# Attention outputs with queries on partitions, and four modulation blocks computed on VectorE instead of TensorE

## The chip, the cores and the metric

The kernel runs on one core of a Trainium2 chip. The core has engines with instruction queues of their own: TensorE (matmuls; the profile shows the loading of stationary operands apart, as PEld), VectorE (DVE), ScalarE (ACT), GpSimd (POOL) and SyncE (SP), which here issues nearly all DMA transfers. SBUF is the on-chip memory with 128 partitions; matmul results land in PSUM, eight banks of 128 x 512 f32. A matmul takes a stationary operand [k, m], loaded first, and streams a moving operand [k, n] past it; the result is [m, n], m on partitions. The metric is the device time of one execution in microseconds, compared by the median of several runs.

## The reference, cut to what matters

Two layers of a diffusion backbone over 1024 latent tokens (a 16 x 64 grid) and 256 context tokens, width 1024, all f32. In each layer adaptive modulation gives six vectors for latents and six for the context (48 tiles of 128 columns, "blocks" 0 to 11 of 512 columns). Then two head groups run on one input projection: a bidirectional mLSTM (8 heads of 64) and neighbourhood attention (8 heads of 64); an output projection and a squared-ReLU MLP follow.

```python
mod = silu_c @ w_ada[l] + b_ada[l]               # and mod_c from silu_cc
sh1, sc1, g1, sh2, sc2, g2 = jnp.split(mod, 6)   # blocks 0-1, 2-3, 4-5, 6-7, 8-9, 10-11
h = rmsnorm(x, norm1_g[l]) * (1 + sc1) + sh1
y = token_mixers(h @ w_in[l], hc @ w_in[l], ...) # mLSTM and attention
x = x + g1 * (y @ w_out[l])
h = rmsnorm(x, norm2_g[l]) * (1 + sc2) + sh2     # blocks 6 to 9 are first needed here
x = x + g2 * (relu(h @ w_mlp1[l]) ** 2 @ w_mlp2[l])
```

In attention each latent query sees a window of 8 rows and 16 columns, with a bias, and all 256 context keys, under one softmax; context queries (layer 0 alone) see the context keys.

```python
s = concat([q @ k_window + bias, q @ k_ctx])
p = softmax(s)                                   # exp(s - max) / sum
y = p_window @ v_window + p_ctx @ v_ctx
```

## The kernel before, in words

**Stages.** `opening` computes modulation blocks 0 to 3 of layer 0 and the first norm. Then, for each layer, `mixers` runs the mLSTM's keys, values and gates, its outputs (`mlstm_out`, tiles of 256 tokens for each of 4 head pairs) and attention (`na`); `outproj`, `up` and `down` follow. Projections are done as three matmuls on f32 numbers split into a high and a low part (`mm3`, L86 to L88).

**Order.** `opening` runs in the order written. Elsewhere the written order gives only the priorities: a scheduler, with estimates of its own for durations, fixes when each instruction is issued, each engine's queue being in order from then on, and hands out tile buffers. A tile name with `bufs=n` has n buffers; a new tile waits for the release of an older one. PSUM has two banks under the name mm and six under q.

**Modulation blocks.** Blocks 6 to 9 of layer 0 come from `ada` (L150): for each of 16 steps (8 slices of k, two column halves), four 32-column stationary tiles of the silu vectors against 256 columns of weights, in four column strips of the array, accumulated in a q bank, with a copy and four transposes (L175) at the end; its 16 transfers have 512 KB. Blocks 4 and 5 come from `ada_rows`: for each 128-column tile of its blocks and each of the two vectors, one 512 KB transfer of weights (L196, into the tile wada, which has one buffer) and one VectorE multiply-and-reduce over 128 x 1024 (L201), and for each vector one transfer (L193) that spreads the silu vector over the partitions. Both are generators. `tick` moves `self.fill` (from `ada`) on by a step, and once that is done, where it is called with True, `self.rows`. It is called in `project_g`, `project2` (False), `project_j` (True) and `mlstm_tile` (True for token tiles 2 and 4).

**Attention.** For each of 4 head pairs (two heads of 64, on 128 partitions), `na_blocks` yields two context blocks of 128 queries (layer 0 only) and eight latent blocks of 128 queries. `na_block` is a generator of three steps for a block:

1. Scores (L844 context keys, L854 window keys), minimum by a VectorE reduction that also negates and adds the bias (L849, L855), exp on ScalarE with its sum (L859), a reciprocal (L860), and the scaling of the 128 x (256 + window) probabilities (L861), for each of the two heads.
2. Transposes of the probabilities, 128 keys at a time or a window's four rows (L869, L880, L888), and copies out of PSUM (L870 ScalarE, L881 VectorE, L889 ScalarE).
3. The output products (L895): the stationary operand is a head's values [keys, 64], the moving one the transposed probabilities [keys, 128 queries]; head 0 writes partitions 0 to 63, head 1 64 to 127, so the result has channels on partitions. `put` copies it on VectorE (L759, L782) into a tile that is stored for the output projection.

`na` calls them so that a new block's step 1 comes after step 2 of the block two before it, then one group of the next head pair's query and key projection (`na_qk`; for the last pair `ahead`, the start of the output projection), then step 3 of that earlier block. Before all that it runs out `self.fill` and `self.rows`.

Of the kernel before, what the change touches and what calls it, by code (L numbers as in the profile page):

```python
# [10 lines left out]
F32 = mybir.dt.float32  # L11
F32R = mybir.dt.float32r
AF = mybir.ActivationFunctionType
ALU = mybir.AluOpType
# [32 lines left out]
class Kern:  # L47
# [698 lines left out]
    def na_blocks(self, l, pr, need_ctx):  # L746
        nc, d, np_ = self.nc, self.d, self.np_
        o = self.nst[pr]
        vs = self.vscr[l]
        v3 = vs[CTX:T, pr * 128:(pr + 1) * 128].rearrange("(r c) e -> r c e", c=GW)  # L750
        k3 = [o["k"][h][:, CTX:T].rearrange("p (r c) -> p r c", c=GW) for h in range(2)]
        yrow = self.yscr[l][512 + pr * 128:512 + (pr + 1) * 128, :]
        if need_ctx:
            yT = np_.tile([128, 512], F32, name="nyT", bufs=2)
            for qt in range(2):
                q = [o["q"][z][0][:, qt * 128:(qt + 1) * 128] for z in range(4)]

                def put(yp, yT=yT, qt=qt):
                    nc.vector.tensor_copy(yT[:, qt * 128:(qt + 1) * 128], yp)  # L759
                    if qt:  # L760
                        nc.sync.dma_start(yrow[:, 0:CTX], yT[:, 0:CTX])

                yield self.na_block(q, None, o["k"], None, None, None, o["vc"], put)
        for hf in range(2):
            R, r0 = NROWS[hf], ROWS0[hf]
            yT = np_.tile([128, 512], F32, name="nyT", bufs=2)
            for cb in range(4):
                c0, w = COLS[cb]
                nl = R * w
                tb = [np_.tile([128, 640], F32, name="S", bufs=SB) for _ in range(2)]  # L770
                for h in range(2):
                    off = self.toff[(hf, cb)] + h * nl
                    nc.sync.dma_start(tb[h][:, CTX:CTX + nl], d["rpbt"][l, pr, :, off:off + nl])
                vt = np_.tile([128, 3, 128], F32, name="vt", bufs=3)
                for lg in range(3):
                    nr = min(4, R - lg * 4)
                    nc.sync.dma_start(vt[0:nr * w, lg, :], v3[r0 + lg * 4:r0 + lg * 4 + nr, c0:c0 + w, :])
                q = [o["q"][z][hf + 1][:, cb * 128:(cb + 1) * 128] for z in range(4)]
                krhs = [k3[h][:, r0:r0 + R, c0:c0 + w] for h in range(2)]

                def put(yp, yT=yT, hf=hf, cb=cb):
                    nc.vector.tensor_copy(yT[:].rearrange("p (r b c) -> p b r c", r=8, b=4)[:, cb, :, :], yp.rearrange("p (r c) -> p r c", r=8))  # L782
                    if cb == 3:
                        nc.sync.dma_start(yrow[:, CTX + hf * 512:CTX + (hf + 1) * 512], yT[:])

                yield self.na_block(q, krhs, o["k"], (R, w), tb, vt, o["vc"], put)
# [26 lines left out]

    def na(self, l, hi, lo, need_ctx, Wq, accs, last):

        run_all(self.fill)
        run_all(self.rows)
        self.wide = 1
        run_all(self.na_qk(l, 0, hi, lo, need_ctx, Wq, accs))
        self.wide = 0  # L820
        pending = []
        for pr in range(4):
            nxt = self.na_qk(l, pr + 1, hi, lo, need_ctx) if pr < 3 else last
            for blk in self.na_blocks(l, pr, need_ctx):
                if len(pending) == 2:
                    next(pending[0])
                next(blk)
                pending.append(blk)
                next(nxt, None)
                if len(pending) > 2:  # L830
                    run_all(pending.pop(0))
            run_all(nxt)
        for blk in pending:
            run_all(blk)

    def na_block(self, q, krhs, k, Rw, tb, vt, vc, put):
        nc, np_ = self.nc, self.np_
        Pn = []
        nl = Rw[0] * Rw[1] if Rw else 0
        mm = nc.tensor.matmul  # L840
        sc = self.bank()
        for h in range(2):
            for z in range(2):
                mm(sc[:, h * CTX:(h + 1) * CTX], q[2 * h + z], k[h][:, 0:CTX], start=z == 0, stop=z == 1, skip_group_check=True)  # L844
        for h in range(2):
            s = tb[h] if nl else np_.tile([128, 640], F32, name="S", bufs=SB)
            m = np_.tile([128, 2], F32, name="smax", bufs=4)
            zb = self.zero[:].to_broadcast([128, CTX])
            nc.vector.tensor_tensor_reduce(s[:, 0:CTX], sc[:, h * CTX:(h + 1) * CTX], zb, -1.0, 3e38, ALU.add, ALU.min, m[:, 0:1])  # L849
            mx = m[:, 0:1]  # L850
            if nl:
                sl = self.bank()
                for z in range(2):
                    mm(sl[:, :nl].rearrange("p (r w) -> p r w", w=Rw[1]), q[2 * h + z], krhs[h], start=z == 0, stop=z == 1)  # L854
                nc.vector.tensor_tensor_reduce(s[:, CTX:CTX + nl], sl[:, :nl], s[:, CTX:CTX + nl], -1.0, m[:, 0:1], ALU.add, ALU.min, m[:, 1:2])  # L855
                mx = m[:, 1:2]
            sm = np_.tile([128, 1], F32, name="ssum", bufs=4)
            sv = s[:, :CTX + nl]
            nc.scalar.activation(sv, sv, AF.Exp, scale=-1.0, bias=mx, accum_out=sm[:])  # L859
            nc.vector.reciprocal(sm[:], sm[:])  # L860
            nc.vector.tensor_scalar(sv, sv, sm[:], None, ALU.mult)  # L861
            Pn.append(s)
        yield
        tiles = []
        tp = self.bank()
        pc = np_.tile([128, 4, 128], F32, name="pc", bufs=2)
        for h in range(2):
            for a in range(2):
                nc.tensor.transpose(tp[:, (h * 2 + a) * 128:(h * 2 + a + 1) * 128], Pn[h][:, a * 128:(a + 1) * 128], self.ident)  # L869
        nc.scalar.copy(pc[:].rearrange("p a t -> p (a t)"), tp[:])  # L870
        for a in range(2):
            tiles.append((128, [vc[:, a, h * 64:(h + 1) * 64] for h in range(2)], [pc[:, h * 2 + a, :] for h in range(2)]))
        if nl:
            R, w = Rw
            pl = np_.tile([128, 4, 128], F32, name="pl", bufs=2)
            tp = self.bank()
            kw = 4 * w
            for h in range(2):
                for a in range(2):
                    nc.tensor.transpose(tp[:kw, (h * 2 + a) * 128:(h * 2 + a + 1) * 128], Pn[h][:, CTX + a * kw:CTX + (a + 1) * kw], self.ident)  # L880
            nc.vector.tensor_copy(pl[:kw].rearrange("p a t -> p (a t)"), tp[:kw, :])  # L881
            for a in range(2):
                tiles.append((kw, [vt[:kw, a, h * 64:(h + 1) * 64] for h in range(2)], [pl[:kw, h * 2 + a, :] for h in range(2)]))
            k3 = (R - 8) * w
            p3 = np_.tile([128, 2, 128], F32, name="pl3", bufs=2)
            tp = yp = self.bank()
            for h in range(2):
                nc.tensor.transpose(tp[:k3, h * 128:(h + 1) * 128], Pn[h][:, CTX + 2 * kw:CTX + nl], self.ident)  # L888
            nc.scalar.copy(p3[:k3].rearrange("p a t -> p (a t)"), tp[:k3, 0:256])  # L889
            tiles.append((k3, [vt[:k3, 2, h * 64:(h + 1) * 64] for h in range(2)], [p3[:k3, h, :] for h in range(2)]))  # L890
        yp = (yp if nl else self.bank())[:, 256:384]
        yield
        for i, (kw, v, pt) in enumerate(tiles):
            for h in range(2):
                mm(yp[h * 64:(h + 1) * 64, :], v[h], pt[h], start=i == 0, stop=i == len(tiles) - 1, skip_group_check=True)  # L895
        put(yp)


    def load_y(self, l, gi, hi, lo, ks=range(KT)):
# [520 lines left out]
    def mixers(self, l, xsrc, hi, lo, need_ctx, W, accs, Wv):  # L1420
        self.wide = 0
        if l == 0:
            for v in range(2):
                self.nc.sync.dma_start(self.sscr[v, :].rearrange("(k p) -> p k", p=128), self.silu[:, :, v])
            self.fill = self.ada(l, range(6, 10), "q")
            self.rows = self.ada_rows(l, range(4, 6), range(2))
        self.gt, self.mst, self.nst = None, {}, {}
        with self.open(name=f"mix{l}", side="right") as self.mx, self.open(name=f"mkv{l}") as self.mp:
            self.cosT = self.load(self.mx, "cos", [128, 8, 32])
# [274 lines left out]
def run_all(g):  # L1704
    for _ in g:
        pass


def chain(*gs):
    for g in gs:  # L1710
        yield from g
# [138 lines left out]
```

## Time and profile before

| | us |
|---|---|
| median of 3 runs | 2898.99 (2896.84 to 2901.7) |
| the profiled execution | 2898.96 |
| its span, first to last instruction | 2897.0 |
| mLSTM of layer 0, about | 100 to 471 |
| attention of layer 0, about | 471 to 700 |
| attention of layer 1, about | 1976 to 2195 |

All rows shown are from that one execution; the clock that TensorE was granted was 0.997 of full over it. The profile's page gives each engine's busy time; views of the trace give busy time in chosen stretches, groups of instructions by line with the minimum, median and maximum duration in ns, waits (who waited for whom, total us, times, longest), and the timeline (start, duration, engine, line, operation, output<-inputs, shapes, count). A matmul's row names stationary shape and then moving shape, so 128*64 128x128 is 64 stationary columns and 128 moving ones on 128 rows; an f32 product that isn't split beforehand shows as two records, one a pass. Names such as q and mm are the PSUM tiles.

### The profile page before, as it was taken

Reading aid. Unit: us, or ns where it says so; the run is one execution under the profiler, and the core shown is the slowest. Engines: PE = TensorE matmul, PEld = TensorE weight load, DVE = VectorE, ACT = ScalarE, POOL = GpSimd, SP = SyncE. Lnnn points to the kernel's source line nnn. Section 1 sums busy time; section 2 is a strip of 40 time slices with the busy share of each in tenths; the row PEclk is TensorE's granted clock in tenths of the full one; section 3 lists DMA queues with packets and bytes.
Section 4 is the critical chain, followed back from the end, with each engine's and each line's share of the span. In section 5 each row is a group of like instructions: output and inputs, shape, how many; then the busy total and the mean of one; then the engine's idle time right before and its main releaser. Section 6 shows DMA issues by size and latency. Waiting matters only on the chain. (4 is left out here: it accounts for less than half of the span.)

```text
span 2897.0 us, 45725 instructions
## 1 busy us (share of the span) xinstructions
PE 2839.9 (98%) x16644; PEld 2405.4 (83%) x16644; DVE 2217.4 (77%) x5097; ACT 1264.8 (44%) x2426; POOL 67.2 (2%) x117
## 2 busy tenths in 40 slices
PE   7999999999999999999999999999999999999998
PEld 4888888888888888888889988888877788888888
DVE  6678987786698777589878778877775887759774
ACT  5333334564563333344545333335564533334443
POOL 0000000001000000000000000000010000000000
PEclk9999999999999999999999999999999999999999
DMA  7433333236447555798977122223356454478673
GB/s 243 155 114 99 121 106 96 86 120 200 155 154 242 194 193 198 249 338 284 328 260 263 65 83 71 77 71 103 94 160 206 131 178 149 156 246 312 216 250 102
DMA packets 278947, 497.42 MB, mean 172 GB/s; under 512 B 23329, under 2 KB 119585, under 8 KB 278721
## 3 DMA queue, kind: packets, MB, share of 16 engines
q1 hardware_dynamic: 278720, 494.49, 51.8%
q8 instruction: 131, 2.15, 0.3%
q14 instruction: 96, 0.78, 0.1%
HBM read 398.82 MB, written 95.59 MB: 171 GB/s over the span
## 5 line engine op out<-in xcount | busy, mean ns | idle before, releaser
L86 PE MATMUL q<-ah,whi 128*128 128x512 f32 (+1 forms) x1488 | 555.1, 373 | 3.3 <-ACT ah L946 2.2
L88 PE MATMUL q<-ah,wlo 128*128 128x512 f32 (+1 forms) x1488 | 553.4, 372 | 1.2 <-DVE wlo L947 1.1
L87 PE MATMUL q<-al,whi 128*128 128x512 f32 (+1 forms) x1488 | 553.9, 372 | 0.0
L86 PE MATMUL mm<-ah,whi 128*128 128x512 f32 (+1 forms) x1104 | 380.0, 344 | 2.1 <-ACT ah L905 2.0
L88 PE MATMUL mm<-ah,wlo 128*128 128x512 f32 (+1 forms) x1104 | 379.0, 343 | 0.5 <-DVE wlo L81 0.5
L87 PE MATMUL mm<-al,whi 128*128 128x512 f32 (+1 forms) x1104 | 379.0, 343 | 0.0
L86 PEld LDWEIGHTS q<-ah,whi 128*128 128x128 f32 x1488 | 280.3, 188 | 53.8 <-ACT ah L946 3.0
L88 PEld LDWEIGHTS q<-ah,wlo 128*128 128x128 f32 x1488 | 280.3, 188 | 51.3 <-DVE wlo L947 2.3
L87 PEld LDWEIGHTS q<-al,whi 128*128 128x128 f32 x1488 | 280.4, 188 | 49.4 <-issue 1.4
L86 PE MATMUL mm<-whi,ah 128*128 128x512 f32 (+2 forms) x864 | 314.0, 364 | 0.6 <-DVE st L312 0.4
L87 PE MATMUL mm<-wlo,ah 128*128 128x512 f32 (+2 forms) x864 | 310.0, 360 | 0.0
L88 PE MATMUL mm<-whi,al 128*128 128x512 f32 (+2 forms) x864 | 309.1, 358 | 0.0
L86 PEld LDWEIGHTS mm<-ah,whi 128*128 128x128 f32 x1104 | 209.0, 189 | 28.3 <-ACT ah L905 2.6
L88 PEld LDWEIGHTS mm<-ah,wlo 128*128 128x128 f32 x1104 | 209.1, 189 | 25.3 <-DVE wlo L81 1.0
L87 PEld LDWEIGHTS mm<-al,whi 128*128 128x128 f32 x1104 | 209.1, 189 | 24.1
L946 ACT CAST ah<-raw 128x512 fp32r<-128x512 f32 (+1 forms) x264 | 143.2, 567 | 123.4 <-PE q L88 57.8
L86 PEld LDWEIGHTS mm<-whi,ah 128*128 128x128 f32 x864 | 164.2, 190 | 27.5 <-issue 3.2
L88 PEld LDWEIGHTS mm<-whi,al 128*128 128x128 f32 x864 | 164.4, 190 | 23.2 <-issue 0.9
L87 PEld LDWEIGHTS mm<-wlo,ah 128*128 128x128 f32 x864 | 164.6, 190 | 21.9 <-issue 0.2
L947 DVE TENSOR_TENSOR al<-raw,ah 128x512 fp32r<-128x512 f32 (+1 forms) x264 | 158.0, 621 | 25.2 <-ACT ah L946 24.8
L947 DVE TENSOR_TENSOR wlo<-raw,whi 128x1024 fp32r<-128x1024 f32 x84 | 102.4, 1222 | 73.6 <-ACT whi L946 71.0
L86 PE MATMUL q<-th,whi 128*128 128x512 f32 x384 | 150.1, 391 | 2.5 <-DVE s L1111 2.3
(284 smaller groups left out, 5253.7 us busy)
## 6 DMA issues: line engine op xcount, KB each, us to landing
raw<-w SPq DMA_DIRECT2D x168, 512.0 KB
raw<-hid SPq DMA_DIRECT2D x104, 512.0 KB
wada<-w_adaT SPq DMA_DIRECT2D x96, 512.0 KB
wraw<-w SPq DMA_DIRECT2D x80, 512.0 KB
hid<-hb SPq DMA_DIRECT2D x128, 256.0 KB
hid<-ht SPq DMA_DIRECT2D x96, 256.0 KB
gb<-gscr SPq DMA_DIRECT2D x36, 512.0 KB
wada<-w_ada SPq DMA_DIRECT2D x32, 512.0 KB
```

The costliest lines, as they stand in the source:

```text
L86: mm(out, lh, rh, start=start, stop=False, skip_group_check=True)
L87: mm(out, lh, rl, start=False, stop=False, skip_group_check=True)
L88: mm(out, ll, rh, start=False, stop=stop, skip_group_check=True)
L946: ins = self.nc.scalar.copy(hi, src)
L947: self.nc.vector.tensor_sub(lo, src, fview(hi))
```

## The change

In `na_block` the scaling of the probabilities is gone: exp writes the two heads' sums into one tile of two columns. In the output products the transposed probabilities are stationary (128 queries) and the values move (64 columns), so the result has queries on partitions and the two heads side by side in columns. VectorE takes the reciprocal of the two sums once and multiplies the 128 x 128 result by them. A fourth step then transposes that tile on TensorE (one 128 x 128 transpose into a new q bank), and `put` copies it from there as before.

`na` keeps up to four blocks alive: step 2 of the block two before, step 1 of the new one, step 4 of the block three before, the projection group, step 3 of the block two before, and a `tick(True)`.

Blocks 6 to 9 leave `ada`: `self.fill` is empty, and `self.rows` is a chain of blocks 4 and 5 and then 6 to 9, all by `ada_rows`, taken on by the ticks of the mLSTM and of attention; what is left is run out after attention instead of before it.

```diff
@@ na
-        run_all(self.fill)
-        run_all(self.rows)
         self.wide = 1
         run_all(self.na_qk(l, 0, hi, lo, need_ctx, Wq, accs))
         self.wide = 0
-        pending = []
+
+        live = []
         for pr in range(4):
             nxt = self.na_qk(l, pr + 1, hi, lo, need_ctx) if pr < 3 else last
             for blk in self.na_blocks(l, pr, need_ctx):
-                if len(pending) == 2:
-                    next(pending[0])
+                if len(live) > 1:
+                    next(live[-2])
                 next(blk)
-                pending.append(blk)
+                live.append(blk)
+                if len(live) == 4:
+                    run_all(live.pop(0))
                 next(nxt, None)
-                if len(pending) > 2:
-                    run_all(pending.pop(0))
+                if len(live) == 3:
+                    next(live[0])
+                self.tick(True)
             run_all(nxt)
-        for blk in pending:
-            run_all(blk)
+        for _ in range(2):
+            next(live[1])
+            run_all(live.pop(0))
+            next(live[0])
+        run_all(live[0])
+        run_all(self.rows)
@@ na_block
+        sm = np_.tile([128, 2], F32, name="ssum", bufs=4)
...
-            sm = np_.tile([128, 1], F32, name="ssum", bufs=4)
             sv = s[:, :CTX + nl]
-            nc.scalar.activation(sv, sv, AF.Exp, scale=-1.0, bias=mx, accum_out=sm[:])
-            nc.vector.reciprocal(sm[:], sm[:])
-            nc.vector.tensor_scalar(sv, sv, sm[:], None, ALU.mult)
+            nc.scalar.activation(sv, sv, AF.Exp, scale=-1.0, bias=mx, accum_out=sm[:, h:h + 1])
...
         for i, (kw, v, pt) in enumerate(tiles):
             for h in range(2):
-                mm(yp[h * 64:(h + 1) * 64, :], v[h], pt[h], start=i == 0, stop=i == len(tiles) - 1, skip_group_check=True)
-        put(yp)
+                mm(yp[:, h * 64:(h + 1) * 64], pt[h], v[h], start=i == h == 0, stop=i == len(tiles) - 1, skip_group_check=True)
+        nc.vector.reciprocal(sm[:], sm[:])
+        y = np_.tile([128, 2, 64], F32, name="ny", bufs=2)
+        nc.vector.tensor_tensor(y[:], yp.rearrange("p (h e) -> p h e", h=2), sm[:].unsqueeze(2).to_broadcast([128, 2, 64]), ALU.mult)
+        yield
+        tp = self.bank()
+        nc.tensor.transpose(tp[:, 0:128], y[:].rearrange("p h e -> p (h e)"), self.ident)
+        put(tp[:, 0:128])
@@ mixers
-            self.fill = self.ada(l, range(6, 10), "q")
-            self.rows = self.ada_rows(l, range(4, 6), range(2))
+            self.rows = chain(*(self.ada_rows(l, blocks, range(2)) for blocks in (range(4, 6), range(6, 10))))
```

More of the change, by code (lines that the diff above doesn't have):

```diff
@@ L756, in na_blocks, with put @@
                 q = [o["q"][z][0][:, qt * 128:(qt + 1) * 128] for z in range(4)]
-                def put(yp, yT=yT, qt=qt):
-                    nc.vector.tensor_copy(yT[:, qt * 128:(qt + 1) * 128], yp)
+                def put(y, yT=yT, qt=qt):
+                    nc.vector.tensor_copy(yT[:, qt * 128:(qt + 1) * 128], y)
                     if qt:
@@ L779, in na_blocks, with put @@
                 krhs = [k3[h][:, r0:r0 + R, c0:c0 + w] for h in range(2)]
-                def put(yp, yT=yT, hf=hf, cb=cb):
-                    nc.vector.tensor_copy(yT[:].rearrange("p (r b c) -> p b r c", r=8, b=4)[:, cb, :, :], yp.rearrange("p (r c) -> p r c", r=8))
+                def put(y, yT=yT, hf=hf, cb=cb):
+                    nc.vector.tensor_copy(yT[:].rearrange("p (r b c) -> p b r c", r=8, b=4)[:, cb, :, :], y.rearrange("p (r c) -> p r c", r=8))
                     if cb == 3:
```

## The prediction, made before the changed kernel had run

> **What bounds the kernel now.** First the page: how busy each engine is over the span.
>
> ```profile
> span 2897.0 us, 45725 instructions
> PE 2839.9 (98%) x16644; PEld 2405.4 (83%) x16644; DVE 2217.4 (77%) x5097; ACT 1264.8 (44%) x2426; POOL 67.2 (2%) x117
> ```
>
> The profiled execution took 2898.96 us, 1.96 us around its span of 2897.0; the median of three runs is 2898.99 (2896.84 to 2901.7). I sum against 2898.96. TensorE is busy 98% of the span, but matmul ends are modelled, so I looked at the two attention stages alone, where nearly all of the change lies: first the busy time of every engine in each, then whom TensorE waited for (first the stage of layer 0, then that of layer 1; total us, times, longest).
>
> ```profile
> core 0: us, PE busy (x) PEld busy (x) DVE busy (x) ACT busy (x) POOL busy (x), PEclk, DMA share, GB/s
> 471.00:700.00 229.00, 222.66 (x1857) 193.55 (x1856) 179.01 (x586) 135.55 (x316) 14.14 (x14) 1.00 0.37 110
> 1976.00:2195.00 219.00, 214.16 (x1680) 182.13 (x1679) 169.92 (x513) 122.47 (x260) 9.23 (x7) 1.00 0.39 119
> ```
>
> ```profile
> PE q L895 <- ACT pl L889: 2.9, 3, 2.0
> PE q L869 <- DVE S L861: 1.1, 1, 1.1
> ...
> PE q L895 <- ACT pl L889: 1.9, 4, 0.7
> ```
>
> TensorE is idle 229.00 - 222.66 = 6.3 us in the first stage and 219.00 - 214.16 = 4.8 us in the second: 11.2 us in 448. VectorE is at 78% and the only wait of TensorE for the normalisation (L861) is 1.1 us. So TensorE sets the pace of attention, and whatever the change takes off VectorE can give back at most about 11 us. What counts is TensorE time per block. A busy matmul overlaps the next, so I price by the distance between starts.
>
> **The output products (L895).** Today the values are the stationary operand (64 columns) and P the moving one (128 columns); the two heads write the two partition halves. Start, duration, engine, line, shapes, records:
>
> ```profile
> 509.15 0.39 PE L88 MATMUL mm<-ah,wlo 128*128 128x512 f32 x1
> 509.47 0.66 PE L895 MATMUL q<-pc,vc 128*64 128x128 f32 x8
> 509.96 0.83 PE L895 MATMUL q<-pl,vt 128*64 128x128 f32 x12
> 510.71 0.66 PE L869 MATMUL q<-consts,S 128*128 128x128 f32 x4
> 511.21 0.49 PE L880 MATMUL q<-consts,S 128*128 128x128 f32 x3
> ...
> 606.08 0.39 PE L88 MATMUL mm<-ah,wlo 128*128 128x512 f32 x1
> 606.40 0.66 PE L895 MATMUL q<-pc,vc 128*64 128x128 f32 x8
> 606.99 0.66 PE L869 MATMUL q<-consts,S 128*128 128x128 f32 x4
> ```
>
> A latent block has 20 records (5 key tiles, 2 heads, 2 passes for f32). From the end of L88's slot (509.15 + 0.23, the spacing of such matmuls) to L869 at 510.71 is 1.33 us. The four transposes behind it take 0.50 instead of the 0.43 that the row at 221.45 below shows, so a latent block's products cost about 1.39 us. A context block (8 records) costs 606.99 - 606.31 = 0.68, with the same tail 0.74. Twenty records in that time means that the heads run side by side: ten slots of 0.11 and some 0.3 us for going into and out of the halved array.
>
> Afterwards P is stationary with 128 columns, the values move with 64, one head after the other. The trace has that shape almost exactly: the mLSTM's numerator, L646, stationary 128x128, moving 65 columns, f32.
>
> ```profile
> 251.59 0.40 PE L88 MATMUL mm<-whi,al 128*128 128x512 f32 x1
> 251.82 1.90 PE L646 MATMUL q<-kva,P 128*128 128x65 f32 x16
> 253.53 0.48 PE L86 MATMUL mm<-whi,ah 128*128 128x512 f32 x1
> 253.85 0.40 PE L87 MATMUL mm<-wlo,ah 128*128 128x512 f32 x1
> ...
> L646 PEld LDWEIGHTS q<-kva,P x576: 186/192/195, 153.9 to 1956.6; 128*128 128x128 f32 x192
> L895 PEld LDWEIGHTS q<-pc,vc x576: 132/137/137, 475.4 to 2193.6; 128*64 128x64 f32 x192
> ```
>
> Sixteen records take 253.53 - 251.82 = 1.71 us, and the next spacing is 0.32 instead of 0.23: (1.71 + 0.09) / 16 = 0.1125 us each, though 65 moving columns are half of 128. The load of 128 stationary columns (192 ns against 137) seems to set that pace, so the halved moving operand buys nothing. Twenty records make 2.25 us, eight 0.90. Layer 0 has 4 head pairs with 8 latent and 2 context blocks, layer 1 4 with 8: 64 latent, 8 context. **64 x (2.25 - 1.39) + 8 x (0.90 - 0.74) = 55.0 + 1.3 = +56.3 us.**
>
> The Trainium skill, page "TensorEngine Tiling (Array Packing)", section "Performance Considerations", advises for a right side of at most 64 columns to swap stationary and streaming operand and tile the columns twofold; that is the form the change gives up. Its factor of up to 2 would make 2.78 us of 1.39 (an estimate), 64 x 0.53 = 34 us more than my sum; the rows say a factor of 1.6, since the halved array has its own entry and exit.
>
> **The transpose back.** Each block gets one 128x128 transpose, 72 in all.
>
> ```profile
> 221.45 0.60 PE L175 MATMUL q<-consts,wada 128*128 128x128 f32 x4
> 221.88 0.78 PE L646 MATMUL q<-kva,P 128*128 128x65 f32 x6
> ```
>
> Four take 0.43 us, one 0.108: **72 x 0.108 = +7.8 us.** It waits for VectorE's reciprocal and multiply (0.16 + 0.29, below), and everything behind it on TensorE's queue, the next projection first, waits too. In the written order the ten transposes and eight score matmuls of two other blocks lie between, some 2.2 us, so near nothing; at the worst all 72 pay 0.45, +32 us. Nearest to the cover: **+1**.
>
> **The normalisation on VectorE.**
>
> ```profile
> L860 DVE RECIPROCAL ssum<-ssum x144: 134/164/167, 472.5 to 2177.0; 128x1 f32<-128x1 f32 x144
> L861 DVE TENSOR_SCALAR S<-S,ssum x144: 340/504/1055, 473.2 to 2177.7; 128x520 f32<-128x520 f32 x32, 128x608 f32<-128x608 f32 x32, 128x544 f32<-128x544 f32 x32, 128x640 f32<-128x640 f32 x32
> L439 DVE TENSOR_TENSOR ropea<-mm,cos x118: 255/284/292, 75.4 to 1947.1; 128x128 f32<-128x128 f32 x118
> ```
>
> Gone: 144 x (0.164 + 0.504) = 96 us. New: 72 reciprocals (0.16) and 72 multiplies of 128x128 out of PSUM, like L439 (0.29): 32 us. That is 64 us off VectorE, and it shortens the way from exp to the transposes by 0.7 us a head. On the end it is worth only what TensorE waits: bounds 0 and -11.2 us; the larger waits are for ScalarE's copy (L889), which stays, but a slower TensorE gives all of them more cover. **-5 us.**
>
> **Blocks 6 to 9 of the modulation.** Removed from TensorE: 128 records on L150 in batches, and four transposes.
>
> ```profile
> 204.78 0.61 PE L646 MATMUL q<-kva,P 128*128 128x65 f32 x4
> 205.32 1.07 PE L150 MATMUL q<-wada,silu 128*32 128x256 f32 x16
> 206.32 0.50 PE L86 MATMUL mm<-whi,ah 128*128 128x512 f32 x1
> 206.66 0.39 PE L87 MATMUL mm<-wlo,ah 128*128 128x512 f32 x1
> ...
> L201 DVE CUSTOM_DVE_ANT_0 wada<-wada,consts x96: 1252/1279/1286, 243.2 to 1617.6; 128x1024 f32<-128x1024 f32 x96
> L201 DVE DVE_READ_ACCUMULATOR2_ANT mod<- x96: 74/82/89, 244.4 to 1618.8; 128x1 f32 x96
> ...
> SPq L196 <- DVE mod L201: 27.5, 9, 5.2
> SPq L777 <- PE q L869: 49.1, 20, 7.7
> ```
>
> Sixteen records run from 204.78 + 4 x 0.1125 = 205.23 to 206.32, 1.09 us, and the next spacing is 0.11 too long: 1.20. Eight such batches and the transposes (0.43) are 10 us. About four batches lie before 125 us, beside the gates' serial scans, where other work may have to fill in; if they were free, 5 us remain. **-9 us.**
>
> Added on VectorE: 32 reductions of 1.28 + 0.08 = 1.36, 43.5 us. The calls count out to 28 steps in the mLSTM (20 joint projections, 8 tiles; the first 17 are for blocks 4 and 5, as now) and 22 in attention, so of the 32 some 10 and 22: 14 us and 30 us. In layer 0's attention VectorE loses 80 x 0.668 = 53 and gains 40 x 0.45 + 30 = 48: it stays near 174 us, in a longer stage, and covers all of it. In the mLSTM the 16 reductions of today lie at 243 to 414 us beside a full TensorE. I cost them at nothing there; if the cover went, each would show its 1.36 us.
>
> Each step also issues one 512 KB transfer on SP, where there were 16; 34 replace them (32 pieces, two broadcast rows). SP takes its queue in order, and a piece waits for the reduction before it (L196 above, between 240 and 471 us: 9 times, up to 5.2 us); behind it stand the bias loads (L777) and values of later blocks. These already wait 49.1 us for buffers in layer 0's attention (the last row) without TensorE waiting for them. Bytes don't bind: 22 pieces are 11.5 MB, in some 130 us 90 GB/s above the 110 of that stage.
>
> **Sum:** +56.3 + 7.8 + 1 - 5 - 9 = +51; 2898.96 + 51 = **2950 us**.
>
> **Rivals.** (a) *The stationary load does not bind for the new products; faster.* If the moving columns alone set the pace, 64 take half of the 0.108 us that 128 take: 0.054 a record, 1.08 for a latent block, 0.43 for a context block. 64 x -0.31 + 8 x -0.31 + 7.8 + 1 - 5 - 9 = -27.5, **2871 us**. It turns the sign below 0.074 a record, where the sum is zero (64 x 20 + 8 x 8 = 1344 records, 94.9 us of products today, 5.2 of the other terms to pay). One row speaks for it, transposes of the opening with 128 stationary and 64 moving columns:
>
> ```profile
> 33.09 0.43 PE L175 MATMUL mm<-consts,arow 64*128 64x64 f32 x4 [0.88 <-DVE arow L172]
> L175 PE MATMUL mm<-consts,arow x8: 222/223/273, 33.1 to 51.5; 64*128 64x64 f32 x8
> ```
>
> The last of four starts 0.43 - 0.22 = 0.21 us after the first: 0.07 each, which would give -6 us. Against it: these are transposes, one pass; L646 is a two-pass product as here. Chance 0.07. The Trainium skill, page "TensorE: Matmul & The Clock Gate", section "Back-to-back issue gap", gives 81 ns per matmul with its load at 128 moving columns; by it the sum would be about +9, 2908 us (an estimate); L646 at 0.1125 disagrees.
>
> (b) *Slower still: the row pieces hold up attention's queues.* A reduction whose piece is late stops VectorE, and the score reductions behind it stop exp and TensorE. For it: the 9 waits of SP above. If each of the 22 steps shows its 1.28 us, +28: **2978 us**. Against: TensorE hardly waited in the mLSTM with the same steps. It decides once a step waits beyond the 5 to 6 us of a projection between two blocks. Chance 0.12.
>
> (c) *The products cost what I say, but every wait goes and planning improves around them*, including the hidden ones in the mLSTM, where a PSUM bank comes free: -10 - 11 and some 20 more would bring 64 + 1 - 41 = +24, **2923 us**. No row shows 20 us to win. Chance 0.05.
>
> **How the numbers follow.** Forecast 0.76. Its own range: low 64 - 10 - 11 = +43, 2942, less 6 for reordering, 2936; high 64 + 8 - 5 = +67, 2966. For 8 in 10 I go to 2930 and, for (b), to 2980; left out are (a), (c) and the ends of the forecast's own cases, some 0.2. Within 0.2% (5.8 us, about what this kernel's measurement can tell): 0.03, from the near ends of (a) and (c); faster, the rest of (a): 0.05; slower: 0.92.
>
> **What would show it.** The output products as 128x128 stationary with 64 moving columns, 1440 minus missing records, spaced 0.112; attention stages longer by about 33 us (layer 0) and 31 us (layer 1) less their waits; the 128-record group on L150 gone and the mLSTM some 9 us shorter; reductions on the row line x128; VectorE in layer 1's attention down by 30 us. I am wrong if the spacing is near 0.06, if the stages don't grow, or if TensorE waits for the back transpose or VectorE by tens of us.

## The result, and the profile after

The changed kernel takes 2950.86 us, median of four runs (2949.73 to 2959.24), against 2898.35 before (four runs): 1.0184 times as long, 95% interval 1.0171 to 1.0197, or +52.5 us. Forecast were 2950, +51. First the page of the changed kernel, then the busy time of every engine in its two attention stages.

```profile
span 2948.7 us, 45551 instructions
PE 2894.1 (98%) x16584; PEld 2489.8 (84%) x16584; DVE 2198.5 (75%) x5012; ACT 1268.7 (43%) x2426; POOL 67.1 (2%) x117
```

```profile
core 0: us, PE busy (x) PEld busy (x) DVE busy (x) ACT busy (x) POOL busy (x), PEclk, DMA share, GB/s
466.00:727.00 261.00, 254.44 (x1896) 237.94 (x1896) 176.09 (x554) 136.42 (x312) 14.12 (x14) 1.00 0.47 146
2000.00:2244.60 244.60, 243.46 (x1715) 224.59 (x1714) 144.90 (x450) 124.95 (x262) 8.95 (x7) 1.00 0.36 107
```

TensorE is as full as before; its stages are longer. VectorE lost 25 us in layer 1's attention (169.92 to 144.90) and 3 us in layer 0's (179.01 to 176.09), where the row pieces (each one 512 KB transfer of weights and one reduction) took the place of the scaling. To place the stages' ends exactly, here are the first and last start of the score matmuls (L844 before, L851 after) and of the output copies, layer 0 and then layer 1; first the kernel before, then the changed one.

```profile
L844 PE MATMUL q<-nk,nqc x32: 277/282/365, 468.6 to 653.7; 128*128 128x256 f32 x32
L782 DVE COPY nyT<-q x32: 271/290/293, 501.9 to 700.1; 128x128 f32<-128x128 f32 x32
L844 PE MATMUL q<-nk,nq x128: 277/282/384, 1976.4 to 2168.1; 128*128 128x256 f32 x128
L782 DVE COPY nyT<-q x32: 272/291/293, 1997.5 to 2194.7; 128x128 f32<-128x128 f32 x32
```

```profile
L851 PE MATMUL q<-nk,nqc x32: 278/283/384, 463.0 to 670.3; 128*128 128x256 f32 x32
L782 DVE COPY nyT<-q x32: 276/284/292, 502.3 to 726.7; 128x128 f32<-128x128 f32 x32
L851 PE MATMUL q<-nk,nq x128: 274/283/388, 2000.5 to 2214.9; 128*128 128x256 f32 x128
L782 DVE COPY nyT<-q x32: 277/284/290, 2025.3 to 2244.4; 128x128 f32<-128x128 f32 x32
```

Attention of layer 0 begins 5.6 us earlier (468.6, 463.0) and lasts 263.7 instead of 231.5 us, +32.2; that of layer 1 lasts 243.9 instead of 218.3, +25.6. These three make -5.6 + 32.2 + 25.6 = +52.2; the rest of the kernel nets to under 1 us.

The output products, in the timeline of the changed kernel:

```profile
494.62 0.39 PE L88 MATMUL mm<-ah,wlo 128*128 128x512 f32 x1
494.84 1.00 PE L900 MATMUL q<-vc,pc 128*128 128x64 f32 x8
495.68 1.50 PE L900 MATMUL q<-vt,pl 96*128 96x64 f32 x12
497.02 0.61 PE L873 MATMUL q<-consts,S 128*128 128x128 f32 x4
497.46 0.60 PE L884 MATMUL q<-consts,S 128*128 128x128 f32 x4
...
L900 PEld LDWEIGHTS q<-vc,pc x576: 186/192/247, 480.6 to 2241.8; 128*128 128x128 f32 x192
```

Twenty records from 494.84 to 497.02, 2.18 us or 0.109 each, and the transposes behind keep their 0.44: no entry and no exit. Before it was 1.39. The loads take 192 ns, as L646's.

### The profile page after: what moved, and what is told of

Read it like the earlier page. It is cut to its first block, busy times and chain, and to the rows that moved or that the text cites. A ratio compares the mean times of both kernels' runs of the same rounds, so it can differ in the third digit from the quotient of the medians.

```text
span 2948.7 us, 45551 instructions
## 1 busy us (share of the span) xinstructions
PE 2894.1 (98%) x16584; PEld 2489.8 (84%) x16584; DVE 2198.5 (75%) x5012; ACT 1268.7 (43%) x2426; POOL 67.1 (2%) x117
## 5 line engine op out<-in xcount | busy, mean ns | idle before, releaser
L201 DVE CUSTOM_DVE_ANT_0 wada<-wada,consts 128x1024 f32<-128x1024 f32 x128 | 163.5, 1278 | 26.0 <-DMA wada<-w_adaT 25.5
```

The source lines that it names most:

```text
L201: nc.vector.tensor_tensor_reduce(raw, raw, row, 1.0, self.bada[l][:, i:i + 1], ALU.mult, ALU.add, mod[:, i, v:v + 1])
```

## The experiments

### The two parts apart

First the row pieces alone, with attention's blocks as before (parts of the edit):

```diff
 mixers
-            self.fill = self.ada(l, range(6, 10), "q")
-            self.rows = self.ada_rows(l, range(4, 6), range(2))
+            self.rows = chain(*(self.ada_rows(l, blocks, range(2)) for blocks in (range(4, 6), range(6, 10))))
 na
-        run_all(self.fill)
-        run_all(self.rows)
...
                 if len(pending) > 2:
                     run_all(pending.pop(0))
+                self.tick(True)
             run_all(nxt)
         for blk in pending:
             run_all(blk)
+        run_all(self.rows)
```

> The kernel before with only blocks 6 to 9 moved to VectorE steps (ticks in the mLSTM and in attention, the rest run out behind attention); attention's blocks as before. Theory: TensorE loses the 10 us of the tiled products, 5 to 10 of them show: 2889 to 2894. Rival (row pieces hold up attention's queues): 22 pieces cost about 1.3 us each there, 2900 or more.

Measured: 2911.94 us against 2899.67, ratio 1.0039 (1.0025 to 1.0053), +12.3. My theory of this part is wrong; the rival is nearer. Stage ends, engines, whom TensorE waited for, in layer 0's attention:

```profile
L844 PE MATMUL q<-nk,nqc x32: 278/283/582, 462.7 to 666.3; 128*128 128x256 f32 x32
L782 DVE COPY nyT<-q x32: 264/286/293, 496.4 to 712.4; 128x128 f32<-128x128 f32 x32
...
463.00:712.70 249.70, 236.04 (x1876) 199.82 (x1876) 206.73 (x640) 138.03 (x319) 14.30 (x14) 0.98 0.49 152
...
PE q L869 <- DVE S L861: 4.5, 4, 1.8
PE q L854 <- DVE smax L855: 1.9, 1, 1.9
PE q L888 <- DVE smax L849: 1.7, 1, 1.7
```

The mLSTM ends 5.9 us earlier, as in the whole change, but the attention stage takes 249.7 instead of 231.5 us: 22 pieces cost 18 us. VectorE is at 83% there. TensorE now waits for the scaling and for the score reductions and is idle 249.70 - 236.04 = 13.7 us, 7 more than before. The granted clock is lower too, 0.98 over the stage, which is 0.02 of 250 = 5 us. The two make 12 of the 18 us; the other 6 lie inside what the profile counts as busy. Four stretches of 10 us in this run:

```profile
510.00:520.00 10.00, 8.13 (x69) 6.60 (x70) 7.09 (x24) 4.54 (x12) 0.00 (x0) 0.97 0.72 226
520.00:530.00 10.00, 9.43 (x73) 7.68 (x74) 7.64 (x19) 6.11 (x13) 0.00 (x0) 0.86 0.45 146
550.00:560.00 10.00, 8.25 (x54) 7.14 (x53) 8.38 (x22) 5.20 (x13) 0.00 (x0) 0.84 0.60 192
590.00:600.00 10.00, 8.11 (x66) 7.07 (x66) 7.77 (x23) 6.66 (x15) 0.00 (x0) 0.89 0.43 136
```

Where TensorE stood for 1.7 to 1.9 us, that stretch of 10 us or the next shows a clock of 0.84 to 0.89; before and in the changed kernel these four stretches have 1.00. So these waits came with a loss beyond their length.

Then the changed attention alone, with the modulation as before (the diff of the change in `na` and `na_block`, without the `tick` and with the two `run_all` ahead):

> The changed attention, blocks 6 to 9 on TensorE as before. Theory: the swapped products and the transposes cost some 57 to 61 us less a few us of waits, 2951 to 2960, slower than the whole change by what the first run gains. Rival (the products are cheap and the row pieces make the loss): 2915 or less.

Measured: 2953.69, ratio 1.0187 (1.0172 to 1.0202), +54.0. The theory holds: attention makes the whole loss, about 27 us in each layer by the rows below. The row pieces, which cost 12 us by themselves, add nothing to it; the whole change lies 1 to 3 us lower, which the intervals don't tell apart.

```profile
L852 PE MATMUL q<-nk,nqc x32: 278/283/387, 468.4 to 671.6; 128*128 128x256 f32 x32
L782 DVE COPY nyT<-q x32: 277/285/292, 507.3 to 727.3; 128x128 f32<-128x128 f32 x32
L852 PE MATMUL q<-nk,nq x128: 274/283/561, 2002.0 to 2218.3; 128*128 128x256 f32 x128
L782 DVE COPY nyT<-q x32: 276/284/290, 2026.9 to 2247.7; 128x128 f32<-128x128 f32 x32
```

Layer 0's attention takes 258.9 us here and 263.7 with the pieces: 22 pieces cost 5 us, not 18. The change gains about as much ahead of attention, which begins at 463.0 instead of 468.4.

### Is it the load of 128 columns?

```diff
             for h in range(2):
-                mm(yp[:, h * 64:(h + 1) * 64], pt[h], v[h], ...)
+                for u in range(2):
+                    us = slice(u * 64, u * 64 + 64)
+                    mm(yp[us, h * 64:(h + 1) * 64], pt[h][:, us], v[h], ...)
```

> The whole change, but each output product split into two with 64 stationary columns (queries 0 to 63 and 64 to 127), which go to the two halves of the array and of PSUM's partitions; moving operand and result as in the change. Theory (the load of 128 stationary columns sets the pace of 0.112 us a record): a pair side by side takes 0.055 to 0.07, a latent block 1.3 to 1.7 us with the entry into the halves instead of 2.19, the whole 2905 to 2925. Rival (a fixed 0.11 us for every pass of 64 columns, whatever is loaded): no gain, 2950 or more.

Measured: 2920.82, ratio to before 1.0076 (1.0061 to 1.0091), 30 us less than the whole change.

```profile
494.98 0.39 PE L88 MATMUL mm<-ah,wlo 128*128 128x512 f32 x1
495.30 0.69 PE L902 MATMUL q<-vc,pc 128*64 128x64 f32 x16
495.81 0.87 PE L902 MATMUL q<-vt,pl 96*64 96x64 f32 x24
496.62 0.65 PE L873 MATMUL q<-consts,S 128*128 128x128 f32 x4
497.11 0.60 PE L884 MATMUL q<-consts,S 128*128 128x128 f32 x4
```

The theory holds. Forty records run from 495.21 (494.98 + 0.23) to 496.62, 1.41 us; with 0.06 more for the transposes behind, which take 0.49 instead of 0.43, that is 1.47, near the 1.39 of the products before. Moving operand, results and arithmetic are those of the change; only the stationary columns are halved and paired. A pass of 64 moving columns has no fixed 0.11 us: 20 pairs in 1.41 us are 0.07 a pair. The rival is out, and the pace goes by the stationary columns. That it is their load, 138 ns here (L902) against 192, is the likely reading; another cost of the full width isn't separated. Of the 64 x (2.18 - 1.47) = 45 us that TensorE's queue lost, 30 came off the end. Layer 1's attention is 20 us shorter than in the whole change, layer 0's only 13: TensorE is idle for 12.8 us there instead of 6.6, and two of its waits are larger than the 1.7 and 1.2 us of the change:

```profile
PE q L908 <- ACT pc L874: 3.7, 3, 2.4
PE q L861 <- DVE nyT L782: 3.4, 1, 3.4
```

L908 is the transpose back, L861 a score product; with less work ahead of them on TensorE the copies on ScalarE and VectorE come late.

### The transpose back

```diff
-        tp = self.bank()
-        nc.tensor.transpose(tp[:, 0:128], y[:].rearrange("p h e -> p (h e)"), self.ident)
-        put(tp[:, 0:128])
+        put(y[:].rearrange("p h e -> p (h e)"))
```

> The whole change without the transpose back: the scaled tile is copied out as it stands, queries on partitions (left out: the transpose, so attention's output is misplaced). Theory: 72 transposes of 0.108 us and the few us that TensorE waits at them, 7 to 13 us less than the whole change: 2938 to 2944. Rival (the wait for VectorE in front of it is the larger loss): 20 us or more, under 2931.

Measured: 2946.32, 4.5 us less than the whole change by the medians, 6 by the ratios to before (1.0163, 1.0148 to 1.0178, whose interval overlaps that of the change). The rival is out, and my theory's 7 to 13 us look too many, though the overlapping intervals don't exclude 7. Three stretches of this run's second attention:

```profile
2145.00:2160.00 15.00, 13.83 (x92) 11.96 (x90) 10.02 (x26) 8.94 (x17) 3.41 (x3) 1.00 0.59 191
2160.00:2175.00 15.00, 15.00 (x103) 14.94 (x104) 8.30 (x31) 8.69 (x20) 1.69 (x2) 0.77 0.55 167
2205.00:2220.00 15.00, 13.43 (x72) 11.82 (x71) 5.80 (x18) 5.56 (x12) 0.00 (x0) 0.89 0.51 163
```

TensorE stands 1.2 and 1.6 us, and the clock after it costs 15 x 0.23 + 15 x 0.11 = 5 us; this attention lasts 246.4 us (1997.2 to 2243.6), longer than the 243.9 with the transposes. That the clock ate the rest is argued from this one profiled execution. Over the four runs the granted clock doesn't order the times: the one with the highest, 0.996, is the slowest, 2947.18.

### What VectorE's scaling is worth

The kernel before without L860 and L861:

> The kernel before without the reciprocal and the scaling of the probabilities, 96 us of VectorE (left out: attention's output stays unnormalised). Theory: TensorE paces attention, so it is worth at most TensorE's idle time, 0 to 11 us, about 5: 2888 to 2899. Rival (VectorE's normalisation paces attention): 20 us or more, under 2880.

Measured: 2898.00 against 2899.67, ratio 0.9994 (0.9985 to 1.0004). No change.

```profile
471.00:700.00 229.00, 223.81 (x1867) 195.03 (x1866) 140.47 (x427) 134.71 (x316) 14.02 (x14) 1.00 0.38 113
```

VectorE falls from 179.01 to 140.47 us in that stage and TensorE's idle time only from 6.3 to 5.2. The same two lines left out of the kernel with the row pieces of the first experiment:

> The kernel before with blocks 6 to 9 as in the first run (22 pieces in attention, 2912), but without reciprocal and scaling of the probabilities (left out: the output stays unnormalised). Theory (the 18 us are VectorE's load: its 22 reductions delay the score reductions): with 53 us off VectorE most of them go, 2894 to 2901. Rival (SP's queue or the transfers' landing holds attention up): still 2907 or more.

Measured: 2901.55 against 2899.14, ratio 1.0013 (1.0003 to 1.0022): 8 us less than with the scaling by the ratios, 10 by the medians, and just above my theory's range. The ends of layer 0's attention say how far the theory goes:

```profile
L844 PE MATMUL q<-nk,nqc x32: 278/283/387, 459.5 to 650.8; 128*128 128x256 f32 x32
L782 DVE COPY nyT<-q x32: 272/292/293, 492.5 to 698.5; 128x128 f32<-128x128 f32 x32
```

The stage lasts 239.0 us, 10.7 less than with the scaling (249.7). But without scaling and without pieces, in the run before this one, it lasts 228.9 (468.4 to 697.3), so 22 pieces still cost 10 us here, where they cost 18 with the scaling. The time of the whole kernel doesn't show it, because attention begins 9 us earlier than in the kernel before. So about 8 of the 18 us were VectorE's scaling. Whether the other 10 are the rest of VectorE's work, the transfers' landing or SP's queue is open. The ends are those of one profiled execution, 2895.73 us, 6 below this median.

### Where else the pieces could go

In the mLSTM alone, two steps a tick, none in attention: first in the changed kernel, by the edit below, then in the kernel before, with the same `tick` and, as in the first experiment, the chain in `mixers` and `run_all(self.rows)` behind attention instead of the two `run_all` ahead.

```diff
 tick
-            next(self.rows, None)
+            for _ in range(2):
+                next(self.rows, None)
 na
-                self.tick(True)
```

> The whole change with two row steps a tick in the mLSTM and none in attention, so that blocks 6 to 9 are done by the mLSTM's end. Attention of layer 0 took 264.3 us with the pieces and 259.5 in the run with the changed attention alone. Theory (pieces cost 5 us in attention, nothing in the mLSTM, where 16 of them cost nothing before): 2943 to 2948. Rival (the mLSTM's VectorE, 83% busy, can't take 32 more reductions): 2951 or more, with TensorE's idle time in the mLSTM up.

Measured: 2986.24, ratio to before 1.0303 (1.0287 to 1.0318), 35 us more than the change.

> The kernel before, blocks 6 to 9 moved to VectorE, all steps in the mLSTM (two a tick), attention untouched. Theory: the 5.6 us by which attention of layer 0 began earlier stay, the 18 us of the pieces in attention go: 2892 to 2897, and it beats both kernels. Rival (the mLSTM pays for the pieces instead): 2900 or more.

Measured: 2930.22, ratio to before 1.0109 (1.0094 to 1.0124), +31. My theory is wrong in both; the mLSTM pays. Its middle, in the kernel before and in the second of these runs, and whom TensorE waited for in that run:

```profile
125.00:440.00 315.00, 312.45 (x1941) 258.15 (x1938) 268.25 (x1027) 104.82 (x286) 16.30 (x35) 1.00 0.37 119
```

```profile
125.00:440.00 315.00, 296.24 (x1643) 241.12 (x1643) 282.23 (x1001) 93.24 (x255) 18.88 (x33) 0.94 0.44 146
...
PE mm L88 <- DVE wlo L82: 6.7, 3, 2.6
PE mm L87 <- DVE ropeb L440: 5.5, 4, 2.3
```

Idle time grows from 2.6 to 18.8 us, and the clock of 0.94 takes 19 us more of 315: together 35 us. That is the delay of attention: with 22 more pieces in the mLSTM it begins at 498.8 instead of 462.7 (the first experiment), and in the changed kernel at 497.5 instead of 463.0. VectorE's busy share alone doesn't tell it: in the changed kernel's row it is as high (281 us against 282), with ten pieces instead of 32 and TensorE hardly waiting.

```profile
125.00:440.00 315.00, 312.73 (x1867) 260.76 (x1868) 281.31 (x1055) 105.19 (x284) 16.54 (x35) 0.99 0.36 115
```

One step at each of the mLSTM's ticks instead, the rest as in the second of these runs:

```diff
 tick
-        if next(self.fill, self) is self and rows:
-            next(self.rows, None)
+        next(self.rows, None)
```

> The kernel before, blocks 6 to 9 moved to VectorE, one step at every tick of the mLSTM (47 of the 50 steps, the False ticks too), instead of two at some, which took 2930. Theory (VectorE's load in the mLSTM is the cause: 32 reductions beside 268 us of work in 315): still 2912 to 2930. Rival (the cause was two steps at once, the second waiting for its transfer): 2900 or less.

Measured: 2914.22, ratio 1.0045 (1.0028 to 1.0062). Within the theory's range; but half of the loss of the run before went, so the pairing, or the places of the ticks, had its share too. Three of the 32 pieces come behind attention here.

```profile
125.00:440.00 315.00, 306.43 (x1801) 254.36 (x1802) 286.13 (x1035) 101.49 (x274) 16.19 (x34) 0.97 0.43 140
```

Last, the kernel before with the 22 pieces that the mLSTM leaves written behind attention (the first experiment without its `tick`):

> The kernel before, blocks 6 to 9 moved to VectorE, one step a tick in the mLSTM as in the change, none in attention's loop; the 22 that are left are written behind attention, so they rank behind its work and fill what VectorE has left there and in the output projection. Theory (what costs is a reduction that comes ahead of score reductions while VectorE is 75 to 90% busy): the tiled products' 6 to 9 us stay gained and attention loses little, 2891 to 2900. Rival (a piece costs wherever it lands, by SP's queue or by the second norm waiting for it): 2905 or more.

Measured: 2921.68, ratio 1.0074 (1.0059 to 1.0089). The rival holds.

```profile
755.00:785.00 30.00, 23.86 (x91) 18.54 (x91) 16.12 (x22) 9.04 (x12) 0.00 (x0) 0.83 0.85 277
815.00:845.00 30.00, 24.16 (x125) 20.69 (x125) 19.50 (x33) 18.32 (x33) 0.00 (x0) 0.89 0.40 139
...
PE mm L268 <- ACT ssq L271: 6.1, 1, 6.1
...
SPq L196 <- DVE mod L201: 39.6, 15, 7.1
```

The 22 pieces share one buffer and run one after the other from 693.9 to 822 us, through the output projection; in the first of these stretches the DMA engines are 85% busy. TensorE stands twice for 6 us at the second norm (L268), and the clock is 0.83 and 0.89 in the two stretches. Attention itself takes what it took before (231.9 us). That the norm's chain waits for these pieces, rather than for the transfers that they delay, isn't separated.

No version that computes the whole output beats the kernel before.

## Why the prediction was right, point by point

The sum was right within 2 us, and its main term was the right one. That it came so near is luck: four terms were off, in both directions, and cancelled. By the stages, products 51, transposes 8, waits -6.5, the modulation -5.6 and the pieces +5 make the 52 that was measured; the last of these had been put at nothing.

- **TensorE sets the pace of attention.** Right. Taking 39 us off VectorE in one stage changed nothing measurable.
- **Products, +56.3.** The halves show that the stationary columns set the pace. The size is 64 x (2.18 - 1.39) = 51 with little for the context blocks: I had carried over L646's exit of 0.09, which is there in front of a split matmul but not in front of transposes. There were 1344 records, as my first rival counts them; the 1440 among the signs was a slip.
- **The rule on tiling.** The Trainium skill's "TensorEngine Tiling (Array Packing)", section "Performance Considerations", was right in direction for this case: the form that it advises was the faster. The "Up to 2×" in the page's "Theoretical Speedup" is 2.18 / 1.39 = 1.57 here. The swap itself isn't needed for it: the products of the change with their stationary columns in halves took 1.47.
- **Transposes, +7.8 and +1 of waiting.** At 0.11 each they are there, and TensorE waited 1.8 us for their input in layer 0 and not in layer 1. Left out, they gave back 4.5 us; the clock may hide the rest, which isn't shown.
- **Waits given back, -5.** TensorE's idle time in the two stages fell from 6.3 + 4.8 to 3.1 + 1.5 us with the changed attention alone, -6.5; in the whole change it is 6.6 + 1.1, the pieces having put 3.5 back in layer 0.
- **The modulation's products off TensorE, -9.** Measured 5.6 at attention's start, near the bound of 5 that I gave. Three of the eight batches, not four, begin before 125 us (88.6, 107.4 and 123.4). In the changed kernel TensorE stands behind them and the clock falls, 15 x 0.11 = 1.7 us (the same stretch before: 1.9 us of waits for the same tile, full clock), as this stretch and its wait show:

```profile
125.00:140.00 15.00, 13.68 (x59) 10.95 (x60) 11.50 (x40) 3.30 (x8) 0.00 (x0) 0.89 0.59 183
...
PE q L516 <- DVE vw L514: 1.9, 1, 1.9
```

Two other runs with the same modulation in the mLSTM have no idle time and full clock in this stretch: the pieces behind attention, where attention begins at 461.8, and the pieces without scaling, at 459.5, 6.8 and 9.1 us earlier than before. So up to the whole 9 was there to win; why the stop came in some runs and not in others isn't shown.
- **Row pieces at nothing.** This step failed. In the changed attention 22 cost 5 us, with the scaling still there 18. I had written that VectorE, near 174 us in the stage, covers all of it; 176 was right, the cover not whole. The price without cover, 1.36 each, was too high in attention (18 / 22 = 0.8) and too low in the mLSTM, where 22 more took 35 us, 1.6 each, half of it clock.
- **Rivals.** (a), the fast one, fell with the first rows: 0.11 a record, not 0.054. (b) was priced for queues; its place, attention of layer 0, was right, its size 5 us instead of 28. Of its cause only the share of VectorE's scaling is shown, 8 of 18 us. (c) did not happen.

The two parts are not additive: +54.0 for attention, +12.3 for the pieces, +52.5 together. The relief of VectorE was worth nothing alone, and to the pieces about 8 us without the scaling and 13 in the change, where TensorE's longer stage covers them too.

## What to carry to other kernels

Where TensorE is full, price a swap of stationary and moving operand by the load of the stationary one: find a row with the same stationary columns, and take the distance between starts, not the duration or the moving columns. Two halves of the stationary operand side by side can do nearly as well as a narrow one: 1.47 us here against 1.39. Work that is moved to an engine with idle time is free only up to some point, which its busy share shows badly: ten pieces in the mLSTM passed with little loss, 22 more cost 35 us, and every microsecond that TensorE then stood came with about another one in its clock. Two parts of a change can need each other, so measure them apart and together.

## What the runs showed of the hardware that I had not expected

Short stops of TensorE went with lost clock. Stretches of 10 to 15 us in which TensorE was idle for 1.2 to 1.9 us, or those right behind them, showed a granted clock of 0.77 to 0.89; over 315 us of the mLSTM 16 us more of idle time came with a mean clock of 0.94. The losses come in like sizes: 15 x 0.11 = 1.7 us and 15 x 0.23 = 3.5 us in the run without transposes back. Not every such stop does it: in the changed kernel the stretch from 510 to 520 us, with 1.2 us idle, and the next have 1.00. What decides it isn't shown.

```profile
510.00:520.00 10.00, 8.82 (x75) 8.58 (x75) 5.92 (x20) 5.22 (x12) 0.00 (x0) 1.00 0.70 213
520.00:530.00 10.00, 10.00 (x88) 9.78 (x87) 8.46 (x29) 6.07 (x13) 0.00 (x0) 1.00 0.63 209
```

The Trainium skill's "TensorE: Matmul & The Clock Gate", Part 1, tells of half the clock after an idle window of about 3.4 us. A loss of 1.7 us agrees with 3.4 us at half the clock; but here single stops of half that length were enough in some places.
